# Loading one row pair of x earlier and moving two block sums in a QKV matrix product

## The chip, the cores and the metric

The kernel runs on 1 core of one Trainium2 chip. The metric is the device time of one execution in microseconds (us); medians over several runs are quoted. Where a ratio with an interval is given, it is the mean time of one kernel's fast runs over the mean of the other's fast runs of the same rounds, so it is not quite the ratio of the medians beside it. Each run also reports the mean clock that TensorE was granted over the whole execution, 1.0 being full speed.

## The reference, cut to what matters

```python
batch, seq, hidden = 16, 512, 768          # x: 8192 rows of 768, w_qkv: 768 x 2304
qkv = np.matmul(x, w_qkv)
q, k, v = qkv[..., :768], qkv[..., 768:1536], qkv[..., 1536:]
return np.stack([q, k, v], axis=0).astype(np.float32)
```

## The kernel before: the parts that matter

The rows of x are worked off in 32 pairs of 128-row blocks. The first two pairs are multiplied with bf16 blocks of the weights while the weights still arrive. From the fourth pair (index 3) on, each pair is two "quads" of seven products each (a scheme of the Strassen kind, which needs sums of weight blocks, `sum_w`, and sums of x blocks, `sums_x`). The third pair (index 2) is a mixture: one quad with products, the other with plain blocks. VectorE works its instructions in program order in these traces (the add at L240 has its input at 43.30 us and starts at 45.21, behind a transpose and two block sums that it doesn't need), and SP or ScalarE (ACT) issue loads and stores in theirs (SP issues the loads of x of the fourth pair at 29.90 us, behind stores issued from 23.77 on).

The path of x of one pair is: four loads of 192 KB (`load_group`), a transpose on VectorE (`transpose`), rounding to bf16 (`round_half` on ACT for the third pair, `round_x` on GpSimd for later ones), and the sums (`sums_x`, on GpSimd).

```python
load_blocks(1, 1)                          # the last weight loads, from SP
for i in range(2):
    load_group(2, i, nc.sync)              # third pair, first half, from SP
# ... (cut: first two pairs; their stores go out from SP)
block(0, 1, bt0, halves(range(4)), cast_next(1, 0, b1[1]))
for i in range(2, 4):
    load_group(2, i, act)                  # third pair, second half, from ACT
block(1, 0, b1[1], halves(range(4)), cast_next(1, 1, bt1))
load_x(3, nc.sync)                         # fourth pair: from SP, behind four stores
# ... (cut)
sum_w(1, 1)
transpose(2)
# ... (cut: the helper round_half)
block(1, 1, bt1, halves(range(4)), round_half)
sums_x(2)
transpose(3)
round_x(3)
sums_x(3)
sum_w(1, 2)
a = quad(2, 0)
# ... (cut)
do(a, 1)
act.activation(b22[0][:], stage[0, 1, 1], ident)
do(a, 2)
rem(2)
sum_w(1, 3)
block(1, 0, b1[1], [(range(KT), (4, )), (range(KT), (5, ))], nothing)
load_x(4, nc.sync)
do(a, 6)
do(a, 5)
block(1, 1, bt1, [(range(KT), (4, ))], nothing)
do(a, 7)                                   # ends in an add on VectorE that reads the bank of product 5
block(1, 1, bt1, [(range(KT), (5, ))], nothing)
do(a, 4)
do(a, 3)                                   # accumulates into that same bank: must wait for the add
store_quad(a)
sum_w(1, 4)
```

Of the kernel before, what the change touches and what calls it, by code (L numbers as in the profile page):

```python
# [10 lines left out]
def kernel(  # L11
# [20 lines left out]
    nc = tc.nc  # L32
    P = 128
# [6 lines left out]
    KH = KT // 2  # L40
    KC = K // 4
    NP = M // (2 * P)
    CB = 512
    REM = N3 - 4 * CB
    Q_OFF = (0, 2 * CB + REM)
    R_OFF = 2 * CB
    fp32 = mybir.dt.float32
    f32r = mybir.dt.float32r
    bf16 = mybir.dt.bfloat16
    ident = mybir.ActivationFunctionType.Identity  # L50
# [12 lines left out]
    st_pool = ctx.enter_context(tc.tile_pool(name="st", bufs=4))  # L63
# [15 lines left out]
    b22 = [w_pool.tile([P, KH, CB], f32r, name=f"b22_{q}") for q in range(2)]  # L79
# [7 lines left out]
    def load_w(dst, j0, nj, off, cols):  # L87
        rows = w_qkv.rearrange("(p j) n -> p j n", j=KT)
        nc.sync.dma_start(dst, rows[:, j0:j0 + nj, off:off + cols])  # L89

    stage = {}

    def load_blocks(q, c, nj=KH):
        if q == 0:
            t = tq_pool.tile([P, KT, CB], fp32, name="st0", tag="tq")
            for j in range(0, KT, nj):
                load_w(t[:, j:j + nj], j, nj, Q_OFF[q] + c * CB, CB)
            stage[q, 0, c], stage[q, 1, c] = t[:, :KH, :], t[:, KH:, :]
        else:
            for h in range(2):  # L100
                t = st_pool.tile([P, KH, CB], fp32, name="st1", tag="st")
                load_w(t[:], h * KH, KH, Q_OFF[q] + c * CB, CB)
                stage[q, h, c] = t[:]

    def sum_w(q, n):
        t1, t2, t3, t4 = ts[q]
        o, in0, in1 = {
            1: (t1, stage[q, 0, 1], stage[q, 0, 0]),
            2: (t2, stage[q, 1, 1], t1),
            3: (t3, stage[q, 1, 1], stage[q, 0, 1]),  # L110
            4: (t4, stage[q, 1, 0], t2),
        }[n]
        nc.vector.tensor_tensor(o, in0, in1, op=sub)  # L113
# [5 lines left out]
    def load_x(p, other):  # L119
        for n in range(2):  # L120
            for h in range(2):
                load_group(p, 2 * h + n, (nc.sync, other)[h])

    def load_group(p, i, eng):
        if p not in xin:
            xin[p] = xin_pool.tile([P, 2 * P // G, KC], fp32, name="xin")
        rows = x_flat[p * 2 * P:(p + 1) * 2 * P, :].rearrange("(g b) k -> b g k", b=G)
        eng.dma_start(xin[p][i * G:(i + 1) * G], rows[:, :, i * KC:(i + 1) * KC])  # L128
# [65 lines left out]
    def quad(p, q):  # L194
        u = Quad()
        u.p, u.q = p, q
        u.o = o_pool.tile([P, 2, 2 * CB], fp32, name="o", tag="o")
        u.x = u.y = u.z = None
        return u

    def product(u, n, ps, start):
        t1, t2, t3, t4 = ts[u.q]
        if n <= 2:
            h = (n - 1) * KH
            lhs = [xb[u.p][:, h + j, :P] for j in range(KH)]
            rhs = [b1[u.q][:, h + j, :] for j in range(KH)]
        else:
            k, t = {3: (4, b22[u.q][:]), 4: (0, t4), 5: (1, t1), 6: (2, t2), 7: (3, t3)}[n]
            lhs = [sr[u.p][:, k, j, :] for j in range(KH)]
            rhs = [t[:, j, :] for j in range(KH)]  # L210
        for j in range(KH):
            nc.tensor.matmul(  # L212
                ps[:], lhs[j], rhs[j],
                start=(start and j == 0), stop=(j == KH - 1), skip_group_check=True,
            )

    def bank():
        return ps_pool.tile([P, CB], fp32, name="ps")

    def do(u, n):  # L220
        c11, c12 = u.o[:, 0, :CB], u.o[:, 0, CB:]
        c21, c22 = u.o[:, 1, :CB], u.o[:, 1, CB:]
        if n == 1:
            u.x = bank()
            product(u, 1, u.x, True)
            nc.scalar.activation(c11, u.x[:], ident)  # L226
        elif n == 2:
            u.z = bank()
            product(u, 2, u.z, True)
            nc.vector.tensor_tensor(c11, c11, u.z[:], op=add)  # L230
        elif n == 6:
            product(u, 6, u.x, False)
            nc.scalar.activation(c12, u.x[:], ident)  # L233
        elif n == 5:
            u.y = bank()
            product(u, 5, u.y, True)
        elif n == 7:
            product(u, 7, u.x, False)
            nc.scalar.activation(c22, u.x[:], ident)  # L239
            nc.vector.tensor_tensor(c22, c22, u.y[:], op=add)  # L240
        elif n == 4:
            product(u, 4, u.x, False)
            nc.scalar.activation(c21, u.x[:], ident)  # L243
        elif n == 3:
            product(u, 3, u.y, False)
            nc.vector.tensor_tensor(c12, c12, u.y[:], op=add)  # L246

    def rows_of(s, p, lo, hi):
        return out_flat[s, p * 2 * P:(p + 1) * 2 * P, lo:hi].rearrange("(r m) n -> m r n", m=P)

    def store_quad(u):
        if u.q == 0:
            nc.sync.dma_start(rows_of(0, u.p, 0, H), u.o[:, :, :H])
            nc.sync.dma_start(rows_of(1, u.p, 0, 2 * CB - H), u.o[:, :, H:])
        else:
            part = 2 * H - Q_OFF[1]
            nc.sync.dma_start(rows_of(1, u.p, H - part, H), u.o[:, :, :part])
            nc.sync.dma_start(rows_of(2, u.p, 0, H), u.o[:, :, part:])
# [8 lines left out]
    def rem(p):  # L267
        ps = ps_pool.tile([P, 2, REM], fp32, name="ps")
        for r in range(2):
            rem_row(p, r, ps[:, r, :])  # L270
        o = or_pool.tile([P, 2, REM], fp32, name="orem")
        nc.scalar.activation(o[:], ps[:], ident)  # L272
        nc.sync.dma_start(rows_of(1, p, R_OFF - H, R_OFF - H + REM), o[:])
# [87 lines left out]
    for h in range(2):  # L361
        load_w(st_rem[:, h * KH:(h + 1) * KH], h * KH, KH, R_OFF, REM)
    load_blocks(0, 1, KH)
    load_blocks(1, 0)
    load_blocks(1, 1)
    for i in range(2):
        load_group(2, i, nc.sync)
    quads = [[quad(p, q) for p in range(NS)] for q in range(2)]

    def busy(n):  # L370
# [13 lines left out]
    def block(q, c, w, groups, cast_next):  # L384



        ps = {}
        for group in groups:
            if callable(group):  # L390
                group()
                continue
            js, tiles = group
            for n in tiles:
                p, r = divmod(n, 2)
                if n not in ps:
                    ps[n] = bank()
                for j in js:
                    nc.tensor.matmul(
                        ps[n][:], xb[p][:, j, r * P:(r + 1) * P], w[:, j, :],  # L400
                        start=(j == 0), stop=(j == KT - 1), skip_group_check=True,
                    )
                if KT - 1 not in js:
                    continue
                if r == 0:
                    cast_next(p)
                u = quads[q][p]
                nc.scalar.activation(u.o[:, r, c * CB:(c + 1) * CB], ps[n][:], ident)
                if c == 1 and r == 1:
                    store_quad(u)  # L410

    def halves(tiles):
        return [(range(h * KH, (h + 1) * KH), tiles) for h in range(2)]

    act, dve = nc.scalar, nc.vector
    def cast_next(q, c, w):
        return lambda p: p < 2 and cast(q, p, c, w, act)
# [42 lines left out]
    for i in range(2, 4):  # L460
        load_group(2, i, act)
    block(1, 0, b1[1], halves(range(4)), cast_next(1, 1, bt1))
    load_x(3, nc.sync)
    t_1 = [tq_pool.tile([P, 2, KH, CB], f32r, name=f"t_1{n}", tag="tq") for n in range(2)]
    ts[1] = [t_1[n // 2][:, n % 2] for n in range(4)]
    sum_w(1, 1)
# [13 lines left out]
    a = quad(2, 0)  # L480
    quads[1].append(quad(2, 1))
    do(a, 1)
    act.activation(b22[0][:], stage[0, 1, 1], ident)
    do(a, 2)
    rem(2)
    sum_w(1, 3)
    block(1, 0, b1[1], [(range(KT), (4, )), (range(KT), (5, ))], nothing)
    load_x(4, nc.sync)
    do(a, 6)
    do(a, 5)  # L490
    block(1, 1, bt1, [(range(KT), (4, ))], nothing)
    do(a, 7)
# [1 line left out]
    do(a, 4)  # L494
    do(a, 3)
    store_quad(a)
    sum_w(1, 4)
    act.activation(b22[1][:], stage[1, 1, 1], ident)

# [43 lines left out]
```

## Time and profile before

| what | value | where |
|---|---|---|
| time, median | 364.63 us (3 runs, 364.61 to 365.05) | run times |
| TensorE busy | 354.6 of 362.4 us | busy shares |
| steady state per pair | 10.74 us of TensorE without a gap | chain that ended last |
| first wait: TensorE for x of the third pair | 1.14 us, ends at 33.89 | timeline |
| second wait: product 3 of the third pair | 1.36 us, ends at 46.03 | timeline |
| TensorE starts the fourth pair | 46.80 us | timeline |

How to read it: "`start, duration, engine, line, operation, out<-in, count [idle before <-releaser]`" is one line of a timeline. The idle time in the brackets is what matters on TensorE, because from the fourth pair on it has no gap left. The lines themselves stand in the prediction below.

### The profile page before, as it was taken

How to read it: one execution, taken by the hardware profiler on the slowest of the kernel's cores; microseconds unless marked ns; L12 is line 12 of the kernel's file. 1: busy time of each engine (PE TensorE's matmuls, PEld its weight loads, DVE VectorE, ACT ScalarE, POOL GpSimd, SP SyncE). 2: the span in 40 equal slices, each digit the busy share in tenths (PEclk: the TensorE clock that was granted, in tenths of full speed). 3: DMA queues.
4: the chain of work that ended last, by engine and by line, in shares of the span. 5: the costliest groups of instructions: out<-in, count | busy, mean ns of one | idle time of the engine just before them, and what ended most of it. 6: DMA issues, size and time to landing. Idle time of an engine off the chain costs nothing.

```text
span 362.4 us, 5237 instructions
## 1 busy us (share of the span) xinstructions
PE 354.6 (98%) x1782; PEld 251.1 (69%) x1782; DVE 224.1 (62%) x233; ACT 186.6 (52%) x308; POOL 178.8 (49%) x185
## 2 busy tenths in 40 slices
PE   8998999999999999999999999999999999999995
PEld 4544567777777777777777777777777777777764
DVE  3583887655666755656765566765566675556643
ACT  4585755454545454444455454545454445454543
POOL 0003676466644456654446664445665445665420
PEclk9999999999999999999999999999999999999999
DMA  7999987889999999999989898898999999999867
GB/s 301 403 375 357 355 282 262 270 299 274 324 304 291 282 290 280 305 310 293 296 272 295 277 326 306 291 275 295 274 322 303 289 289 281 289 293 316 292 238 256
DMA packets 81450, 108.09 MB, mean 298 GB/s; under 512 B 4880, under 2 KB 61456, under 8 KB 81424
## 3 DMA queue, kind: packets, MB, share of 16 engines
q1 hardware_dynamic: 65472, 95.96, 81.0%
q10 hardware_dynamic: 15952, 11.80, 9.8%
q8 instruction: 14, 0.23, 0.2%
q14 instruction: 12, 0.10, 0.1%
HBM read 32.24 MB, written 75.50 MB: 297 GB/s over the span
## 4 chain that ended last, share of the span: by engine, by line
PE 85%; DMA 8%; DVE 1%; SPq 1%; issue 1%; ACT 1%; ACTq 0%; DVEq 0%
PE ps L212 75%; PE ps L262 10%; DMA st<-in_w_qkv_dram 5%; DMA xin<-in_x_dram 3%; DVE t L113 1%; SPq L128 1%; SPq L89 0%; ACT o L243 0%; ACTq L303 0%; ACT b L380 0%; SPq L143 0%; ACT orem L317 0%; DVE o L240 0%; DVE o L230 0%; ACTq L319 0%
## 5 line engine op out<-in xcount | busy, mean ns | idle before, releaser
L212 PE MATMUL ps<-t,s 128*128 128x512 f32 x708 | 177.7, 399 | 0.0
L212 PEld LDWEIGHTS ps<-t,s 128*128 128x128 f32 x708 | 133.0, 188 | 30.5
L175 POOL CAST xb<-xf 128x1536 bf16<-128x1536 f32 x29 | 43.8, 1510 | 132.9 <-DVE xf L132 132.9
L240 DVE TENSOR_TENSOR o<-o,ps 128x512 f32<-128x512 f32 x59 | 40.5, 687 | 91.2 <-ACT o L239 91.2
L132 DVE STREAM_TRANSPOSE xf<-xin 128x1536 f32<-128x1536 f32 x30 | 88.6, 2955 | 8.5 <-DMA xin<-in_x_dram 8.5
L212 PE MATMUL ps<-b,xb 128*128 128x512 bf16 x354 | 86.4, 380 | 1.1 <-ACT xb L472 1.1
L212 PEld LDWEIGHTS <-xb 128*128 128x128 bf16 x354 | 32.1, 98 | 38.0 <-issue 7.6
L239 ACT ACTIVATE o<-ps 128x512 f32<-128x512 f32 x59 | 35.3, 598 | 44.4 <-PE ps L212 44.3
L233 ACT ACTIVATE o<-ps 128x512 f32<-128x512 f32 x59 | 35.3, 598 | 42.3 <-PE ps L212 39.5
L246 DVE TENSOR_TENSOR o<-o,ps 128x512 f32<-128x512 f32 x59 | 40.5, 687 | 22.5 <-PE ps L212 21.4
L212 PE MATMUL ps<-b,s 128*128 128x512 f32 x177 | 49.6, 389 | 1.4 <-DVE o L240 1.4
L226 ACT ACTIVATE o<-ps 128x512 f32<-128x512 f32 x59 | 35.2, 597 | 24.8 <-DVE o L246 21.5
L243 ACT ACTIVATE o<-ps 128x512 f32<-128x512 f32 x59 | 35.3, 598 | 24.2 <-PE ps L212 21.3
L183 POOL TENSOR_TENSOR s<-xf 128x384 fp32r<-128x384 f32 x30 | 31.8, 1059 | 31.8 <-DVE xf L132 31.8
L262 PE MATMUL ps<-w_rem,xb 128*128 128x256 bf16 x384 | 47.2, 273 | 0.0
L262 PEld LDWEIGHTS <-xb 128*128 128x128 bf16 x384 | 37.4, 98 | 11.2 <-issue 0.5
L212 PEld LDWEIGHTS ps<-b,s 128*128 128x128 f32 x177 | 33.1, 188 | 8.6 <-issue 1.8
L230 DVE TENSOR_TENSOR o<-o,ps 128x512 f32<-128x512 f32 x59 | 37.2, 673 | 2.0 <-ACT o L226 1.3
L184 POOL TENSOR_TENSOR s<-s,xf 128x384 fp32r<-128x384 f32 x30 | 30.4, 1013 | 2.3
L187 POOL TENSOR_TENSOR s<-xf,s 128x384 fp32r<-128x384 f32 x30 | 30.4, 1013 | 0.0
L185 POOL TENSOR_TENSOR s<-xf 128x384 fp32r<-128x384 f32 x30 | 30.3, 1011 | 0.0
L272 ACT ACTIVATE orem<-ps 128x512 f32<-128x512 f32 x31 | 18.5, 598 | 20.0 <-PE ps L262 20.0
(35 smaller groups left out, 120.7 us busy)
## 6 DMA issues: line engine op xcount, KB each, us to landing
out_dram<-o SPq DMA_DIRECT2D x62, 768.0 KB, 4.9
out_dram<-o SPq DMA_DIRECT2D x65, 256.0 KB, 4.1
xin<-in_x_dram SPq DMA_DIRECT2D x64, 192.0 KB, 6.9
xin<-in_x_dram ACTq DMA_DIRECT2D x56, 192.0 KB, 4.5
out_dram<-orem SPq DMA_DIRECT2D x31, 256.0 KB, 5.8
st<-in_w_qkv_dram SPq DMA_DIRECT2D x6, 768.0 KB, 11.1
xin<-in_x_dram SPq DMA_DIRECT2D x2, 768.0 KB, 4.8
st<-in_w_qkv_dram SPq DMA_DIRECT2D x6, 256.0 KB, 5.9
```

Of the source, the lines that this page charges most:

```text
L132: nc.vector.transpose(t[:].rearrange("p j (g b) -> p g j b", b=G), xin.pop(p)[:].rearrange("p g (a j) -> p g j a", a=G),)
L175: nc.gpsimd.tensor_copy(out=xb[p][:], in_=xf[p][:])
L183: g.tensor_tensor(s[:, 1], a21, a22, op=add)
L212: nc.tensor.matmul(ps[:], lhs[j], rhs[j], start=(start and j == 0), stop=(j == KH - 1), skip_group_check=True,)
L226: nc.scalar.activation(c11, u.x[:], ident)
L230: nc.vector.tensor_tensor(c11, c11, u.z[:], op=add)
L233: nc.scalar.activation(c12, u.x[:], ident)
L239: nc.scalar.activation(c22, u.x[:], ident)
L240: nc.vector.tensor_tensor(c22, c22, u.y[:], op=add)
L243: nc.scalar.activation(c21, u.x[:], ident)
L246: nc.vector.tensor_tensor(c12, c12, u.y[:], op=add)
L262: nc.tensor.matmul(ps, xb[p][:, j, r * P:(r + 1) * P], w_rem[j // KH][:, j % KH, :], start=(j == 0), stop=(j == KT - 1), skip_group_check= ...
```

## The change

The intent: x of the fourth pair should be there by the time the transpose of the third ends, so that VectorE does both back to back, is not late for the add before product 3, and two of the block sums and a copy on ACT are taken out of the same stretch.

```diff
@@ first loads
     for i in range(2):
         load_group(2, i, nc.sync)
+    load_x(3, nc.sync)
@@ after the blocks of the first two pairs
     block(1, 0, b1[1], halves(range(4)), cast_next(1, 1, bt1))
-    load_x(3, nc.sync)
@@ third pair
     do(a, 1)
-    act.activation(b22[0][:], stage[0, 1, 1], ident)
     do(a, 2)
     rem(2)
-    sum_w(1, 3)
     block(1, 0, b1[1], [(range(KT), (4, )), (range(KT), (5, ))], nothing)
     load_x(4, nc.sync)
     do(a, 6)
+    act.activation(b22[0][:], stage[0, 1, 1], ident)
     do(a, 5)
@@ end of the third pair
     store_quad(a)
+    sum_w(1, 3)
     sum_w(1, 4)
```

(A small helper is split off without effect. It moves line numbers: the add called L240 before is L243 after, L132 becomes L135, and so on.)

More of the change, by code (lines that the diff above doesn't have):

```diff
@@ L100, in load_blocks, with load_half @@
             for h in range(2):
-                t = st_pool.tile([P, KH, CB], fp32, name="st1", tag="st")
-                load_w(t[:], h * KH, KH, Q_OFF[q] + c * CB, CB)
-                stage[q, h, c] = t[:]
+                load_half(q, h, c)
+    def load_half(q, h, c):
+        t = st_pool.tile([P, KH, CB], fp32, name="st1", tag="st")
+        load_w(t[:], h * KH, KH, Q_OFF[q] + c * CB, CB)
+        stage[q, h, c] = t[:]
     def sum_w(q, n):
```

## The prediction

> **What bounds the kernel now.** I read the page's busy shares first: TensorE (PE) is busy 354.6 of 362.4 us at full granted clock, so all idle time of PE together is 7.8 us, or 2.1% of the span. That is the first bound on any schedule change. Part of those 7.8 us is the start and the tail, which this change does not touch. Then I read the chain that ended last in order of time. From 46.03 us on it is PE alone; before that it runs through loads of x and through VectorE (DVE):
>
> ```profile
> PE 354.6 (98%) x1782; PEld 251.1 (69%) x1782; DVE 224.1 (62%) x233; ACT 186.6 (52%) x308; POOL 178.8 (49%) x185
> ...
> 22.87 6.97 DMA xin<-in_x_dram
> ...
> 32.28 5.21 DMA xin<-in_x_dram
> ...
> 40.56 1.79 DVE t L113
> 42.35 0.60 DVE o L230
> 42.94 2.34 DVE t L113
> 45.28 0.61 DVE o L240
> 45.89 0.14 issue
> 46.03 2.24 PE ps L212 x9
> 48.27 1.31 PE ps L262 x12
> 49.58 9.44 PE ps L212 x42
> 59.02 1.31 PE ps L262 x12
> ```
>
> The first load is the second half of x of the third pair (row blocks are counted in pairs, and the third has index 2); the last of x of the fourth pair (index 3) is at 32.28. A pair in the steady state costs 9.44 + 1.31 = 10.74 us of PE with no gap, to the end of the kernel. So what the change can move is the moment at which PE begins the fourth pair, 46.80 us, and any gap that it opens in that pair. The timeline of PE and DVE shows the gaps before it:
>
> ```profile
> 33.89 1.47 PE L212 MATMUL ps<-b,xb 128*128 128x512 bf16 x6 [1.14 <-ACT xb L472]
> 37.61 3.10 DVE L132 STREAM_TRANSPOSE xf<-xin 128x1536 f32<-128x1536 f32 x1 [4.65 <-DMA xin<-in_x_dram]
> 42.80 2.49 DVE L113 TENSOR_TENSOR t<-st,st 128x1536 fp32r<-128x1536 f32 x1
> 45.21 0.68 DVE L240 TENSOR_TENSOR o<-o,ps 128x512 f32<-128x512 f32 x1
> 46.03 0.93 PE L212 MATMUL ps<-b,s 128*128 128x512 f32 x3 [1.36 <-DVE o L240]
> ```
>
> There are two. PE waits 1.14 us for x of the third pair (loaded, transposed, rounded), and 1.36 us before product 3 of that pair, because the add at L240 must read the bank first. That add is late because DVE works in order: the transpose of the fourth pair could only start when its x landed at 37.5, and behind it stand two block sums (L113). The second gap is what the change aims at.
>
> [...]the sum beside GpSimd's work took 2.49 us, an undisturbed one about 1.75, and GpSimd's tensor operation beside it 2.51 instead of 1.00. [...]the two loads issued from ScalarE (ACT) at 22.44 and 22.87 moved no byte in 24 to 26 us, when the SP queue alone moved packets, and had 65% of the engines' time in 26 to 28. It looks like one line in order of issue. [...]I use the order of issue, as a reading of this trace.
>
> **The change part by part.**
>
> *The load.* The four loads of 192 KB leave their place behind the stores (issued from 29.90 on) and go behind the first half of the third pair. Nothing is added in bytes. The SP queue was held back there: its issues came at 16.59, 18.58, 21.92, 23.77 and 26.38, each just after an older weight load had landed. If the four x loads take the next of these places, two are issued before ACT's loads at 22.44 and 22.87 and two behind. Before, two 256 KB stores stood in those two places. So ahead of the critical half of the third pair 0.39 MB take the place of 0.52 MB; but the x loads are in small packets, which moved at 295 GB/s in 24 to 26 us against about 400 for the others: 1.3 us for either. I expect the third pair's x to land within some tenths of where it did (29.84), with 0.2 us of delay as my middle. The fourth pair's x, last issued near 26.4 plus 5 to 6 us to landing, is there by 32 to 33 us instead of 37.5, about when the transpose before it ends (32.96).
>
> *DVE in the third pair.* Transpose 30.0 to 33.0, transpose of the fourth pair to 36.0, sum 2 to about 37.9, L230 to about 39.3 (its product ends later than it used to matter). L240 then waits for ACT alone: ACT's L239 ended at 43.3, so L240 ends near 44.0. Product 4 of three matmuls started at 43.62; at 0.68 us (the spacing of such groups from 55.51 on) PE is ready for product 3 at 44.3 instead of 46.03. **Gain: 1.7 us.** The b22 copy moved on ACT (1.5 us) lies at 40.6 to 42.1, where ACT was idle 1.41 us; it is needed at 44.3. It costs nothing.
>
> *The two sums behind the third pair.* They do not vanish. Sum 3 is first needed by product 7 of the fourth pair's second quad, some 7 us later, so that is in time. But DVE is in order, and now, from the start of the fourth pair (call it T), it does L246 (done at T + 0.8, as before: 47.60 - 46.80), two sums of 1.73 (undisturbed, since GpSimd's sums should then be done: 9.4 us of its work before became 6 undisturbed), the next transpose of 2.93 and two L230 of 1.28 together: T + 8.5; then L240, about 0.6, and 0.14 to PE: T + 9.24. PE wants product 3 of the first quad at T + 8.71 (55.51 - 46.80). **Cost: 0.5 us** of a new wait, in the fourth pair. Before, DVE had one sum (2.19) there, and L240 ended at T + 8.2. Afterwards DVE has some 3.7 us of slack per pair (10.74 less 2.95 and six adds of about 0.68), so nothing of it accumulates.
>
> *Sum:* -1.7 + 0.2 + 0.5 = -1.0 us on 364.63, giving 363.7 rounded (0.3%).
>
> **The rivals.**
>
> *A load delays a load.* If all four loads get ahead of the critical half of the third pair, 0.79 MB at 280 to 295 GB/s put it 2.7 to 2.8 us later, less the 1.3 us of the stores they replace: PE's wait at 33.89 grows by 1.4 us, and everything behind it. That eats the gain: about 364.9 with the new wait. For it: order of issue seems to rule, and small packets are slow. Against: SP's issues came no faster than older loads landed.
>
> *Stores late, buffers late.* With four more loads ahead, the stores of the first output quads start up to 6 us later (29.5 instead of 23.8). The third pair's second quad writes into the buffer of the first one, from 38.7 us; the first quad's last store would land at about 36, by 30 plus 6. Two us of margin; if it fails, ACT's eviction and a PSUM bank wait, 1 or 2 us: 365 to 366.
>
> *The wait moves whole.* If the sums take 2.2 to 2.5 us again, through GpSimd, the new wait in the fourth pair is 1.5 to 2 us and the result is 364.6 to 365: same to a few tenths. For it: in the kernel before both late sums were stretched. Against: GpSimd should be ahead by then.
>
> *Everything hidden:* DVE catches up and only the gain stands: 362.9.
>
> **Range and chances.** The middle is 363.7. The low end, 362.7, is the full 1.7 us with the load landing a little earlier. The high end, 365.2, is the first or the third rival with some tenths on top. The three runs before spread by 0.44 us, small beside it. For faster by over 2% the kernel would have to lose 7.3 us, while the two gaps on the path hold 2.5 us by the profile: 1%. For slower by over 2% the stores would have to stop PE for over 7 us: 1%. Within 2%: 98%.
>
> **What would show it right or wrong.** In the timeline of the changed kernel: the fourth pair's transpose directly behind the third's, from about 33 instead of 37.61; the 1.36 us before product 3 gone or under 0.2; product 3 near 44.5 and the fourth pair's start near 45.3 instead of 46.80; PE's wait near 33.9 at 1.0 to 1.6 us; two sums of 1.73 back to back after L246; a new idle of PE of about 0.5 us before product 3 of the fourth pair, released by L240. From there on every piece of the chain is 10.74 us again. I would be wrong if the first half-load lands over 1 us later, if ACT waits for a store at its evictions near 38, or if the sums beside GpSimd take over 2.2 us.

## The result, and the profile after

The changed kernel takes 366.18 us in the median (6 runs, 365.68 to 367.61) against 364.62 (6 runs, 364.42 to 365.05). The ratio of the fast runs is 1.0045, interval 1.0028 to 1.0063: within 2%, but slower by 1.6 us where I had forecast 1.0 us faster, and outside my range. Its six runs report clocks of 0.991 to 0.995, where the profiled execution before reports 1.0.

The timeline of TensorE in the changed kernel, third and fourth pair:

```profile
35.31 1.50 PE L215 MATMUL ps<-b,xb 128*128 128x512 bf16 x6 [2.88 <-ACT xb L475]
36.61 2.76 PE L265 MATMUL ps<-w_rem,xb 128*128 128x256 bf16 x12
39.16 3.19 PE L403 MATMUL ps<-b,xb 128*128 128x512 bf16 x12
...
47.59 0.85 PE L215 MATMUL ps<-b,s 128*128 128x512 f32 x3
48.28 1.47 PE L215 MATMUL ps<-b,xb 128*128 128x512 bf16 x6
...
57.41 0.94 PE L215 MATMUL ps<-b,s 128*128 128x512 f32 x3 [0.27 <-DVE o L243]
```

The second wait, the aim of the change, is gone: the line at 47.59 has no bracket. But the first wait has grown from 1.14 to 2.88 us, and then comes something that I had no step for: the twelve matmuls with 256 columns at 36.61 take 2.55 us to the next line, instead of 1.31 (35.20 to 36.51 in the kernel before). The same twelve matmuls, the same data. The view of busy time by stretch, whose column PEclk is the granted clock (columns: stretch, its length, busy time of PE, PEld, DVE, ACT, POOL with counts, PEclk, DMA share, GB/s), says why:

```profile
36.50:37.00 0.50, 0.50 (x4) 0.29 (x2) 0.50 (x1) 0.50 (x2) 0.50 (x2) 0.61 1.03 391
37.00:39.50 2.50, 2.50 (x13) 1.66 (x11) 2.50 (x3) 1.47 (x4) 2.50 (x2) 0.50 1.07 406
39.50:40.00 0.50, 0.50 (x2) 0.15 (x1) 0.32 (x1) 0.50 (x1) 0.50 (x2) 0.50 1.01 412
40.00:41.00 1.00, 1.00 (x6) 0.50 (x5) 0.00 (x0) 0.05 (x1) 1.00 (x2) 0.99 1.08 399
```

TensorE ran at half clock from about 36.6 (the first stretch averages 0.61, so 0.78 of its 0.5 us were at half) to about 40.0: 3.4 us, which lose 1.7 us of work. The kernel before shows 1.00 in every stretch from 27 to 49 us. The 3.41 us before the fall (33.20 to 36.61) hold 2.11 us of the wait of 2.88; the section on the clock below sets that beside the other profiled executions.

Why the first wait grew, first in the chain of waits of the changed kernel (start, us, what), then on VectorE's timeline:

```profile
22.54 8.74 DMA xin<-in_x_dram
```

```profile
31.48 5.78 DVE L135 STREAM_TRANSPOSE xf<-xin 128x1536 f32<-128x1536 f32 x2 [5.17 <-DMA xin<-in_x_dram]
46.41 0.69 DVE L243 TENSOR_TENSOR o<-o,ps 128x512 f32<-128x512 f32 x1 [6.59 <-ACT o L242]
49.08 1.75 DVE L116 TENSOR_TENSOR t<-st,st 128x1536 fp32r<-128x1536 f32 x1
50.75 1.75 DVE L116 TENSOR_TENSOR t<-st,t 128x1536 fp32r<-128x1536 f32 x1
```

The last load of x of the third pair took 8.74 us from its issue at 22.54; before it took 6.97 from 22.87. The two transposes now are back to back ("x2"), as intended, but begin at 31.48 instead of 30.03. (Kernels with the same loads in the same places began at 30.03 and 30.34, or at 31.23 to 31.80, each in one profiled execution, so some tenths of such a difference are chance.) VectorE then idles 6.59 us before the add: the place that was crowded has become empty.

Where the 2.0 us between the two profiled executions (spans 362.4 and 364.4 us) come from, step by step on TensorE:

| piece | before | after | difference |
|---|---|---|---|
| TensorE resumes after the first wait at | 33.89 | 35.31 | +1.42 |
| from there to product 3 | 12.14 | 12.28 | +0.14 |
| product 3 to the fourth pair | 0.77 | 0.69 | -0.08 |
| fourth pair | 10.75 | 11.29 | +0.54 |
| sum | | | +2.02 |

The second row hides two large terms. In a run of another kernel below with the same early load and full clock, this piece took 10.62 us (10.60 in the changed kernel itself with its first wait filled). So the wait that the change removed gave 12.14 - 10.62 = 1.52 us, and the half clock took 12.28 - 10.62 = 1.66 us back.

How fast the loads moved, by the view of DMA in the same stretch from 27 to 28 us, first the kernel before, then the changed one (q1 is SP's queue, q10 ACT's):

```profile
DMA packets 320, 0.28 MB, mean 280 GB/s; under 512 B 17, under 2 KB 301, under 8 KB 320
q10 hardware_dynamic: 288, 0.21, 86.1%
q1 hardware_dynamic: 32, 0.07, 25.1%
```

```profile
DMA packets 302, 0.22 MB, mean 220 GB/s; under 512 B 15, under 2 KB 302, under 8 KB 302
q10 hardware_dynamic: 246, 0.18, 94.8%
q1 hardware_dynamic: 56, 0.04, 18.2%
```

The loads of x are of packets of 768 bytes (192 columns of 4 bytes), and in this stretch of the changed kernel, where nothing else moves, the 16 engines carry some 300 of them per us: 0.22 MB per us, with the engines busy throughout. At 22 to 23 us, when weights with packets of 2 KB moved, it was 416 GB/s in both kernels. The packet size alone is not the reason: in the best kernel below, 419 packets, by their bytes about 373 of them of 768, moved from 29 to 30 us (311 GB/s), and in the kernel before 451 from 26 to 27 us, when stores of 1 KB packets ran beside loads of x.

### The profile page after: what moved, and what is told of

Its sections match the earlier page's. It is cut to its first block, busy times and chain, and to the rows that moved or that the text cites. A ratio compares the mean times of both kernels' runs of the same rounds, so it can differ in the third digit from the quotient of the medians.

```text
span 364.4 us, 5233 instructions
## 1 busy us (share of the span) xinstructions
PE 355.7 (98%) x1782; PEld 251.2 (69%) x1782; DVE 223.4 (61%) x233; ACT 186.6 (51%) x308; POOL 176.3 (48%) x185
## 4 chain that ended last, share of the span: by engine, by line
PE 87%; DMA 7%; DVE 3%; ACT 1%; SPq 1%; ACTq 0%; issue 0%; DVEq 0%
PE ps L215 74%; PE ps L265 11%; DMA st<-in_w_qkv_dram 5%; DMA xin<-in_x_dram 2%; DVE xf L135 2%; PE ps L403 2%; DVE t L116 0%; SPq L89 0%; ACT o L246 0%; ACTq L306 0%; DVE o L233 0%; SPq L146 0%; ACT xb L475 0%; ACT orem L320 0%; ACT b L384 0%
## 5 line engine op out<-in xcount | busy, mean ns | idle before, releaser
L178 POOL CAST xb<-xf 128x1536 bf16<-128x1536 f32 x29 | 42.5, 1464 | 136.1 <-DVE xf L135 136.1
L243 DVE TENSOR_TENSOR o<-o,ps 128x512 f32<-128x512 f32 x59 | 40.5, 689 | 96.4 <-ACT o L242 96.4
L135 DVE STREAM_TRANSPOSE xf<-xin 128x1536 f32<-128x1536 f32 x30 | 88.3, 2948 | 5.2 <-DMA xin<-in_x_dram 5.2
L265 PE MATMUL ps<-w_rem,xb 128*128 128x256 bf16 x384 | 48.5, 277 | 0.0
L246 ACT ACTIVATE o<-ps 128x512 f32<-128x512 f32 x59 | 35.3, 598 | 24.8 <-PE ps L215 21.9
L186 POOL TENSOR_TENSOR s<-xf 128x384 fp32r<-128x384 f32 x30 | 30.4, 1014 | 33.2 <-DVE xf L135 33.2
L188 POOL TENSOR_TENSOR s<-xf 128x384 fp32r<-128x384 f32 x30 | 30.5, 1017 | 0.0
L275 ACT ACTIVATE orem<-ps 128x512 f32<-128x512 f32 x31 | 18.5, 597 | 20.1 <-PE ps L265 19.0
```

What stands on the lines that cost most here:

```text
L135: nc.vector.transpose(t[:].rearrange("p j (g b) -> p g j b", b=G), xin.pop(p)[:].rearrange("p g (a j) -> p g j a", a=G),)
L178: nc.gpsimd.tensor_copy(out=xb[p][:], in_=xf[p][:])
L243: nc.vector.tensor_tensor(c22, c22, u.y[:], op=add)
L246: nc.scalar.activation(c21, u.x[:], ident)
L265: nc.tensor.matmul(ps, xb[p][:, j, r * P:(r + 1) * P], w_rem[j // KH][:, j % KH, :], start=(j == 0), stop=(j == KT - 1), skip_group_check= ...
```

## The experiments

Theory after the result: three terms. (1) The fourth pair's loads, in small packets, share the DMA engines with the third pair's and make them land 1.4 us later. (2) The longer idle time makes TensorE's clock fall to one half for 3.4 us. (3) The moved sums cost half a us in the fourth pair. The rivals: that the sums alone are to blame; that the matmuls are slow because of the traffic beside them; that the loads from ACT are late for another reason. In the edits, "after" means that the kernel started from is the changed one. Every kernel gave correct output; the matmuls on zeros go to a bank that nobody reads.

Each of the three batches below had its own runs of the kernel before on the same chip, 11 per batch: medians 364.60, 364.36 and 364.73 us. The three chips are different ones, so between batches I compare differences to these medians. A profile is one execution of a kernel.

### The sums moved, the load not

```diff
 (after)
-    load_x(3, nc.sync)          # early
+    load_x(3, nc.sync)          # back behind block(1, 0, ...)
```

> The kernel before with the two block sums and the b22 copy moved as in the change, x of the fourth pair loaded where it was. My theory (the late load costs the gain, the moved sums are nearly neutral or good): TensorE's first wait stays at 1.1 us, the clock stays 1.00, product 3 of the third pair starts near 44.3 instead of 46.0, and the fourth pair opens a wait of 0.4 us if GpSimd is done, up to 1.5 us if its sums collide with the block sums: 363.3 to 364.4 us. Rival (the moved sums are what makes the changed kernel slow): 366 us or more.

Measured: 364.22 us (364.10 to 364.31), clock 0.998 to 1.0 in all five runs; ratio 0.9983, interval 0.9966 to 1.0000. The rival falls: the moved sums do not make the kernel slow. The first wait was 1.76 us and not the 1.1 of my expectation (x landed 0.3 us later than before, though its loads are unchanged). The second wait is gone here without any earlier load, since product 3 starts right behind product 4 (44.79): from the end of the first wait to product 3 are 10.60 us, as with the load alone below. Either part of the change is enough to remove it. But a new wait stands in the fourth pair, larger than in the changed kernel, since a block sum takes 2.56 us instead of 1.75 while GpSimd is busy (4.00 of the 4.00 us from 46 to 50). The timeline of TensorE, and of VectorE ahead of it:

```profile
55.45 0.93 PE L215 MATMUL ps<-b,s 128*128 128x512 f32 x3 [1.11 <-DVE o L243]
```

```profile
47.95 2.56 DVE L116 TENSOR_TENSOR t<-st,t 128x1536 fp32r<-128x1536 f32 x1
```

### The load moved, the sums not

```diff
 (before)
         load_group(2, i, nc.sync)
+    load_x(3, nc.sync)
 ...
-    load_x(3, nc.sync)
```

> The kernel before with only the load of x of the fourth pair moved ahead. My theory: first wait of TensorE again about 2.9 us, then about 3.4 us of half clock, no wait for L240 before product 3, and no new wait in the fourth pair, so 0.4 us below the changed kernel: 365.8 us. Rival (the sums are to blame): back to 364.6 us or below.

Measured: 365.44 us in the median, but in two groups: 363.90 us at a clock of 0.999 (once, the profiled run), and 365.37 to 365.74 at 0.994 or 0.995 (five times). One kernel, two times, 1.5 us apart. The profiled run fell in the faster group, which I had not expected; it shows what the loads alone do. The timeline of TensorE:

```profile
35.26 1.47 PE L212 MATMUL ps<-b,xb 128*128 128x512 bf16 x6 [2.90 <-ACT xb L472]
36.57 1.47 PE L262 MATMUL ps<-w_rem,xb 128*128 128x256 bf16 x12
37.88 2.75 PE L400 MATMUL ps<-b,xb 128*128 128x512 bf16 x12
```

The first wait is the same as in the changed kernel (2.90 us) and comes from the load alone. This time the clock did not fall, and the twelve matmuls at 36.57 take 1.31 us again, although the same loads and stores run beside them. This is the run from which the 10.62 us above are taken (35.26 to 45.88).

### The changed kernel with the first wait filled

```diff
 (after)
     block(1, 1, bt1, halves(range(4)), round_half)
+    busy(12)                    # 12 matmuls on zeros, result unused
```

> The changed kernel with 12 matmuls on zeros (2.6 us) put into TensorE's first wait; the result is unused, the output stays right. Theory A (the half clock follows from the idle time itself): clock 1.00 throughout, the first wait's end stays at about 35.3 us, and the time falls by half of 3.4 us, 1.7 us: 364.5 us. Rival B (the matmuls of the third pair are slow for another reason, memory traffic of loads and stores beside them): they stay slow and the time stays at 366.2 us.

Measured: 364.54 us (364.27 to 364.83), clock 0.998 to 1.0 in all five runs. The x of the third pair comes as late as in the changed kernel (TensorE resumes at 35.66), the twelve matmuls take 1.31 us again (timeline of TensorE), yet the kernel is 1.6 us faster with 12 matmuls more. The rival of slow matmuls by traffic falls. So without the half clock the change as a whole is worth nothing: -0.06 us against the kernel before of the same batch.

```profile
36.97 1.47 PE L265 MATMUL ps<-w_rem,xb 128*128 128x256 bf16 x12
38.28 2.54 PE L403 MATMUL ps<-b,xb 128*128 128x512 bf16 x11
```

### The load alone with the first wait filled

The edit is the same `busy(12)` on the load-only kernel.

> The load moved alone (the one that ran at 363.9 us once at full clock and at 365.4 to 365.7 us five times at a clock of 0.995) with 12 matmuls on zeros in TensorE's first wait. Theory (the two times of that kernel are one half-clock stretch): all runs at a clock of 0.998 or more and 363.8 to 364.2 us. Rival (the two times have another cause that the clock only follows): times of 365.4 us remain in some runs.

Measured: 363.75 us (363.64 to 363.89), all six runs at 0.997 to 1.0. The slower group is gone; the two times of the load-only kernel were one half-clock stretch. This kernel is 0.61 us below the kernel before of its batch; the one with the sums moved (filled as well) was 0.06 below its own. The difference, 0.55 us, is what the moved sums cost once the load is early.

### The changed kernel with four matmuls in the wait

The edit is `busy(4)` instead of `busy(12)`.

> The changed kernel with only 4 matmuls on zeros (0.9 us), leaving about 2.1 us of idle time, as in the run with the third pair first, in which 5 of 6 runs had the half clock. Theory (the length of the idle stretch decides): most runs at a clock near 0.995 and 366 us, some at full clock and 364.5 us. Rival (it is enough that TensorE does something in between): all at full clock and 364.5 us, as with 12.

Measured: 364.58 us; one run of six at half clock (366.17 us, 0.995), five at full clock (364.21 to 364.76). A miss for my count: I had said most. The profiled run was the slow one: there the half clock (granted clock 0.54 from 36 to 38 us) came behind an idle stretch of 2.11 us. The idle stretches of the other five are not on record, so why they kept the full clock isn't shown; the section on the clock gives an estimate of the reason.

### All of the third pair from SP, ahead of the fourth

```diff
 (after)
-    for i in range(2):
+    for i in range(4):
         load_group(2, i, nc.sync)
     load_x(3, nc.sync)
 ...
-    for i in range(2, 4):
-        load_group(2, i, act)
```

> The changed kernel with all four loads of x of the third pair issued from SP ahead of those of the fourth, none from ScalarE. My theory (loads are served in the order of issue, and small packets of x move at 220 GB/s): the third pair's x lands near 29.0 us instead of 31.3 (29.84 before), TensorE's first wait is 0.4 to 1 us, the clock stays 1.00, the gain of 1.7 us before product 3 stands, and the fourth pair's wait of 0.4 us stays: 362.3 to 363.0 us. Rival (ScalarE's loads were not held up by the fourth pair's; the delay has another cause): landing stays near 31.3 us and the time at 366.2 us.

Measured: 365.40 us; one run at 363.77 (clock 0.998), five at 365.31 to 365.55 (0.993 to 0.995). This missed its expectation. The third pair's x was now issued from 14.0 to 20.1 us, wholly ahead of the fourth's, and its transpose still began only at 30.84 (31.48 in the changed kernel, 30.03 before), with a first wait of 2.16 us. So strict order of issue, my reading in the prediction, looks wrong: loads that are issued behind others seem to slow these down. The next two runs test that. VectorE:

```profile
30.84 5.77 DVE L135 STREAM_TRANSPOSE xf<-xin 128x1536 f32<-128x1536 f32 x2 [4.49 <-DMA xin<-in_x_dram]
```

### All of the third pair from SP, the fourth late as before

```diff
 (before)
-    for i in range(2):
+    for i in range(4):
         load_group(2, i, nc.sync)
 ...
-    for i in range(2, 4):
-        load_group(2, i, act)
```

> The kernel before with all four loads of x of the third pair issued from SP (the second half no longer from ScalarE); x of the fourth pair late and the sums in place as before. Theory A (x of the third pair comes late because small packets of the fourth pair's x share the DMA engines with it): here nothing of the fourth pair is beside it and the two 256 KB stores now come behind it, so it lands near 29.0 us, TensorE's first wait is under 0.6 us, clock 1.00; the 1.7 us before product 3 stay lost, so 364.0 to 364.4 us. Rival B (issuing from SP is itself the slow way): landing at 30.5 us or later and a wait over 1.7 us.

Measured: the third pair's transpose began at 29.36, 1.48 us earlier than in the run above, and the first wait fell to 0.86 us. The third pair's loads are the same in both kernels and stand in the same places; up to that time only what is issued behind them differs, small-packet loads of x there, stores here. So theory A holds for the landing as far as the fourth pair's loads go (that their packets are small is not shown to be the reason: the stores behind were of 1 KB packets), and issuing from SP is not the slow way. Each figure is from one execution; with stores behind, two further profiles below began at 29.58 and 30.00, so the delay is 0.8 to 1.5 us. The time did not follow: 366.42 us in the median, two runs at full clock (364.60 and 364.91) and four at 0.995 (366.41 to 366.53). TensorE was early, but the fourth pair's x was as late as ever (its transpose at 38.34), so all of the gain came back as a longer second wait, of 2.68 us, and this time the half clock came behind that one (granted clock 0.61 from 46 to 50 us). Timelines of VectorE and TensorE:

```profile
29.36 2.95 DVE L132 STREAM_TRANSPOSE xf<-xin 128x1536 f32<-128x1536 f32 x1 [3.09 <-DMA xin<-in_x_dram]
```

```profile
46.69 1.43 PE L212 MATMUL ps<-b,s 128*128 128x512 f32 x3 [2.68 <-DVE o L240]
47.92 2.65 PE L212 MATMUL ps<-b,xb 128*128 128x512 bf16 x6
```

The last line takes 2.49 us to the next group (50.41) instead of 1.31. The half clock follows the long idle stretch: here the one of 2.68 us before product 3, in the changed kernel the one of 2.88 us before the third pair.

### All of the third pair from SP, the fourth behind two stores

```diff
 (before)
-    for i in range(2):
+    for i in range(4):
         load_group(2, i, nc.sync)
 ...
     for p in range(2):
         rem(p)                  # each ends in a 256 KB store from SP
+    load_x(3, nc.sync)
 ...
-    for i in range(2, 4):
-        load_group(2, i, act)
 ...
-    load_x(3, nc.sync)
```

> As the run before it, but x of the fourth pair goes directly behind the two 256 KB stores of the remainder columns, ahead of the output stores; sums in place. Theory A: the third pair's x lands near 29.0 to 29.5 us, the fourth's near 33 us; first wait under 1 us, no wait before product 3, clock 1.00 in all runs: 362.3 to 362.9 us, ahead of both kernels. Rival B: the third pair's x lands at 30.5 us or later and the time is 363.7 us or, in runs with a half-clock stretch, 365.4 us.

Measured: 362.08 us (361.91 to 362.67), clock 0.998 to 1.0 in all six runs; ratio 0.9935 to the kernel before, interval 0.9920 to 0.9950. It beats both kernels, by 2.3 us and 4.1 us by the medians, and is a little faster than I had expected. The timeline of TensorE, then that of VectorE:

```profile
33.45 1.47 PE L212 MATMUL ps<-b,xb 128*128 128x512 bf16 x6 [0.90 <-ACT xb L470]
44.05 0.85 PE L212 MATMUL ps<-b,s 128*128 128x512 f32 x3
44.74 1.47 PE L212 MATMUL ps<-b,xb 128*128 128x512 bf16 x6
```

```profile
29.58 2.93 DVE L132 STREAM_TRANSPOSE xf<-xin 128x1536 f32<-128x1536 f32 x1 [3.32 <-DMA xin<-in_x_dram]
33.12 3.02 DVE L132 STREAM_TRANSPOSE xf<-xin 128x1536 f32<-128x1536 f32 x1 [0.60 <-DMA xin<-in_x_dram]
```

Two 256 KB stores between the two pairs' loads keep the fourth out of the third's way (29.58) and still bring it at 33.12, 0.6 us after VectorE could have used it. The second wait is gone, the fourth pair starts at 44.74 instead of 46.80, and no sum had to be moved for it.

### The best kernel with the sums moved as in the change

The edit is the third and fourth part of the diff of the change (without the load), on the kernel above.

> The kernel with the fourth pair's x behind the two remainder stores, with the two block sums and the b22 copy moved as in the change. Theory (moving the sums costs a new wait of 0.4 to 0.6 us in the fourth pair and gains nothing once the load is early, since VectorE idles in the third pair): 362.5 to 362.7 us. Rival (the moved sums help): 361.9 us or less.

Measured: 362.96 us (362.60 to 363.22), all at full clock; 0.3 us above my expectation, on a chip on which the kernel before is 0.4 us slower. Against the kernels before of their batches that is -1.77 us, and -2.28 for the same kernel without the moved sums: the moved sums cost 0.5 us here too. Their wait shows in the fourth pair, as in the changed kernel:

```profile
54.28 0.94 PE L212 MATMUL ps<-b,s 128*128 128x512 f32 x3 [0.27 <-DVE o L240]
```

The bracket understates it: from the fourth pair's start to product 3 of its first quad are 9.13 us here (45.15 to 54.28) and 8.70 in the kernel above (44.74 to 53.44).

### An idle stretch made by other means

```diff
 (the best kernel; round_half of the third pair)
-    act.activation(xb[2][:, :, rows], xf[2][:, :, rows], ident)
+    for _ in range(4 if r == 0 else 1):
+        act.activation(xb[2][:, :, rows], xf[2][:, :, rows], ident)
```

> The kernel with the fourth pair's x behind the two remainder stores (362.08 us, always at full clock, first wait 0.90 us), in which ScalarE writes the first rounded row of the third pair four times instead of once, so that TensorE waits some 2.25 us longer, 3.1 us in all. All loads and stores are as in that kernel. Theory (an idle stretch of about 3 us is what halves the clock, whatever its cause): most runs show a clock near 0.995 and take 362.1 + 2.25 + 1.7 = 366.0 us. Rival (in the changed kernel it was the traffic of loads beside the matmuls): full clock in all runs and 364.3 us.

Measured: 366.67 us (365.92 to 367.75), all six runs at a clock of 0.991 to 0.995. The wait became 3.74 us, more than the 3.1 that I had worked out, which explains 0.6 us of the excess over the expected 366.0. No load or store was issued in another order here, and the half clock comes all the same.

```profile
36.12 2.45 PE L212 MATMUL ps<-b,xb 128*128 128x512 bf16 x6 [3.74 <-ACT xb L471]
38.37 2.22 PE L262 MATMUL ps<-w_rem,xb 128*128 128x256 bf16 x12
```

> The run before it with 12 matmuls on zeros (2.6 us) in the lengthened wait. Theory: full clock in all runs, 364.3 us. Rival (ScalarE's extra work is what costs, not the clock): no change against the run before it.

With `busy(12)` in that wait: 365.02 us (364.79 to 365.22), all six runs at 0.997 to 1.0. It is 1.65 us faster by the medians: the half clock again, with ACT's extra work unchanged. That it is 0.7 us above my expectation is the longer wait.

### What the runs say of the clock together

The longest idle stretch of TensorE is from each profiled execution (the start-up of the kernel left out); "half clock" counts runs with a mean clock of 0.995 or less; the others are all at 0.997 or more.

| kernel | longest idle stretch, us | half clock |
|---|---|---|
| load alone, 12 matmuls in the wait | under 0.2 | 0 of 6 |
| changed, 12 matmuls in the wait | 0.51 | 0 of 5 |
| best kernel | 0.90 | 0 of 6 |
| best kernel, sums moved | 1.15 | 0 of 6 |
| before | 1.36 | 4 of 33 |
| idle by other means, 12 matmuls in the wait | 1.41 | 0 of 6 |
| sums moved alone | 1.76 | 0 of 5 |
| changed, 4 matmuls in the wait | 2.11 | 1 of 6 |
| third pair first | 2.16 | 5 of 6 |
| third pair from SP, fourth late | 2.68 | 4 of 6 |
| changed | 2.88 | 6 of 6 |
| load alone | 2.90 | 5 of 6 |
| idle by other means | 3.74 | 6 of 6 |

The order is plain: in the kernels with up to 1.76 us of idle time in one piece the half clock is rare (4 of 67 runs), in those with 2.11 us and more it is common (27 of 36).

The traces show more. The trace file of a profile records the stretches of the granted clock (the column PEclk is worked out from them). In the changed kernel they are: full from 5.89 us for 30.72 us, half from 36.61 for 3.413 us, full from 40.03 for 324.27 us, then half in the tail, where TensorE has no work left. In the kernel before: full from 7.21 for 354.99 us, then half in the tail. The three full stretches are 9.0, 95.0 and 104.0 times the 3.413 us of the half one. Of the four other profiled executions with a half clock I have PEclk in stretches of 2 to 4 us. Three add up to 3.40 us of it: third pair first (from about 35.28), four matmuls in the wait (from about 36.16), idle by other means (from about 36.48). The fourth, the third pair from SP and the fourth late, has 3.1 us of it, from about 46.9 to the end of that view at 50 us; its twelve matmuls from 50.41 on take 1.31 us, as at full clock. In all five executions the 3.41 us right before the fall hold over 2 us of TensorE's idle time: 2.11 in the changed kernel, 2.16, 2.11, 3.05 and 2.68 in the other four. In the kernel before, cut into lengths of 3.413 us from 7.21 on, none holds more than 1.27 before the tail.

The length of the wait alone doesn't decide: the load alone kept the full clock in its profile (1.00 from 20 to 60 us) with 2.90 us of idle time in one piece. An estimate of mine, from the three multiples and the five falls: the clock changes only at whole multiples of 3.413 us from the first record of full clock (5.89 us in one trace, 7.21 in the other), and the idle time since the last such moment counts. The 2.90 us could then have fallen on both sides of one. That isn't shown, since the moments of that execution are not on record here. Shown is that one kernel comes out at half clock in some runs and not in others (the load alone in 5 of 6).

The four slow runs of the kernel before (366.17 to 366.53 us) were not profiled, so that theirs is the same half clock is only suggested by clock and time.

## Why the prediction was wrong, point by point

**What bounds the kernel, and where the change can act: right.** TensorE alone carries the chain from the fourth pair on, before and after, and the whole difference was made before 60 us.

**The load: wrong, in size.** The step that failed reads: "I expect the third pair's x to land within some tenths of where it did (29.84), with 0.2 us of delay as my middle." It landed at 31.28 us, 1.44 later. The places in SP's queue were as I had said: the fourth pair's four loads were issued at 18.73, 21.84, 23.69 and 27.22, two ahead of ACT's at 22.11 and 22.54 and two behind. Two figures were off. I had used 295 GB/s for small packets from a stretch in which stores were mixed in; x alone moved at 205 to 231 in the changed kernel. At 220 GB/s the 0.39 MB ahead take 1.8 us instead of 1.3: an estimate of 0.5 us of the delay. And I had let the order of issue rule, so that the loads behind would cost nothing; from 28 to 29 us ACT's queue and SP's moved at once in the changed kernel (74.5% and 36.5% of the engines' time), and the run with the third pair first against the one with the fourth late shows 1.5 us of delay by loads issued wholly behind (0.8 to 1.5 with the other two profiles). I had a rival for this ("A load delays a load"), sized at 1.4 us, and TensorE resumed 1.42 later (its wait grew by 1.74, since it also ran dry 0.3 us earlier). That the size fits is partly luck: the rival put all four loads ahead at 280 to 295 GB/s, and two came ahead, slower, and two behind. I gave it too little weight.

**The second wait: right.** Predicted gain 1.7 us, measured 1.52 at full clock; the rest is the step from product 4 to product 3, 0.89 us where I took 0.68. Not seen: either part of the change alone brings this gain, so the two together can't add up. The b22 copy on ACT cost nothing that any trace shows.

**The moved sums: right.** Predicted 0.5 us of a new wait before product 3 of the fourth pair, released by L240 (L243 after), with two undisturbed sums of 1.73 back to back after L246. Measured: two sums, 1.67 us from start to start, and a fourth pair longer by 0.54 us; in pairs of kernels 0.55 and 0.5 us. (A slip without effect: the 9.4 us of GpSimd's work before are five of its six instructions; all six took 10.4.)

**The clock: a term that the sum lacked.** I wrote that TensorE was "at full granted clock" and carried that over. None of my steps or rivals let the clock depend on the wait. The half clock cost 1.66 us in the trace, and 1.6 us by the median when the wait was filled with matmuls. Shown: the filling takes it away in three kernels (changed, load alone, idle by other means), an idle stretch of 3.74 us made on ACT brings it (six runs of six), and in the five profiled executions with the half clock the 3.41 us before the fall hold 2.11 to 3.05 us of idle time. The sum with measured terms is 1.42 - 1.52 + 1.66 + 0.54 - 0.08 = +2.02 us, the difference of the two spans. Had I put my own rival's 1.4 us into the sum instead of 0.2, the forecast would have been 0.2 us over the kernel before; the clock makes the rest.

**The other rivals.** "Stores late, buffers late": the first output store was indeed issued at 31.35 us instead of 23.77, but no trace shows a wait for its buffer. "The wait moves whole": not in the changed kernel, where GpSimd was ahead; but it is what the sums moved alone showed, with 2.56 us for one sum beside GpSimd and a wait of 1.11 us.

**What stays open.** Why a load issued behind others on the same queue slows them down isn't settled, nor whether it matters that these were loads and not stores. Neither the 768 bytes of the packets nor the 32 partitions that each such load fills is alone the reason of the 220 GB/s, since loads of the same form moved at 311 GB/s from 29 to 30 us in the best kernel; what makes the difference isn't shown. Nor is it shown when a load on another queue gets its turn: in the kernel before, ACT's two loads, issued at 22.44 and 22.87 us, moved nothing from 24 to 26 us, and from 26 to 27 us ACT's queue had 44.4% of the engines' time beside 64.7% of SP's. How much idle time halves the clock is not known either: 2.11 us within the 3.41 before a fall was enough, 1.27 was the most without one in the kernel before, and the load alone kept the full clock with 2.90 us in one piece. For the runs without a profile the idle times aren't on record: why it was one run of six in one kernel and five of six in another is not shown.

## What to carry to other kernels

Before you move a load ahead, ask what is on its way at that moment that TensorE needs first, and at what rate such transfers move side by side (here x alone at 205 to 231 GB/s, weights at 416), not only how many bytes they are; a couple of large stores between them can be worth more than the earlier place (here, with two of 256 KB between the pairs, the third pair's transpose began at 29.58 us instead of 30.84). A wait on TensorE had two prices here: its own length and, in the kernels with 2.11 us and more in one piece, in 27 of 36 runs a stretch at half clock, which cost another 1.7 us. And when one kernel shows two times in unchanged conditions, sort its runs by the granted clock before you explain anything; filling a wait with idle matmuls is a cheap test, and sometimes a cure (1.6 us in the changed kernel).
